# Third mixer of a four-mixer block: weight low parts on GpSimd, key factors in the second memory round, residual rescaling in four parts

## The chip, the cores and the metric

The kernel runs on one core of a Trainium2 chip. The metric is the device time of one execution in microseconds (us). TensorE is PE in the profile, VectorE DVE, ScalarE ACT, GpSimd POOL, SyncE SP.

## The reference

Two blocks of two layers each work on one sequence of 512 tokens with 1024 features, all in float32. The first block has an RG-LRU mixer, a stick-breaking attention, and a SwiGLU feed-forward after each. It ends in an RMS norm with the gain `final_g`. The second block has two gated mixers. The change lies in the first of these, the third mixer of the whole, whose reference is, cut to what matters:

```python
h = rmsnorm(x, norm_gain[l])
mk, mv = jnp.split(memn @ w_mem_kv[l], 2, axis=-1)            # 256 memory rows, 4 heads of 128
qa, ka, va, qb, kb, vb, qm, gate = split_cols(h @ w_in_even[e], SPLIT_EVEN)
qa = rope_2d(rmsnorm(qa, q_norm_a[e]), grid_row, grid_col)    # 8 heads of 64
ka = rope_2d(rmsnorm(ka, k_norm_a[e]), grid_row, grid_col)    # 2 heads of 64
ya = global_gqa(qa, ka, va)                                   # all 512 keys
yb = window_gqa(qb, kb, vb, sink_b[e], rel_bias)              # 128 keys to each side
ym = memory_attn(qm, mk, mv)
y = jnp.concatenate([ya, yb, ym], axis=-1) * jax.nn.silu(gate)
x = x + y @ w_out_even[e]
```

Two things in it matter here. The norm of queries and keys is per head: its sum over 64 features gives one factor for each token and head, by which the keys are scaled before the scores. And the `x` of the residual is the first block's normed output, while the mixer's projections start before that norm's factors are known.

## The kernel before

Activations stand with features on the 128 partitions: a tile is 128 features by 512 tokens, and eight tiles hold one activation. To keep float32 accuracy, each operand of a product is split into a high part (rounded to fp32r) and a low part (the rest), and a product is three matmuls: high by high, high by low, low by high (`mm3`, L169 to L171). One 512-column matmul of each kind follows another.

Weights come in chunks of 128 by 512 (`fetch`): SP issues a load (L149), ACT rounds the high part `wh` (L150), and DVE subtracts to get the low part `wl` (L151). There are six slots of each (`N_W`), and a chunk is fetched five ahead of its use. A projection of 128 output features takes two chunks and 24 matmuls. In the third mixer the weights' key is ("we_m", column): column 0 is the keys `ka`, 1 to 4 the queries `qa`, 5 the window attention's keys `kb`, 6 to 9 its queries `qb`, 10 to 13 the memory queries `qm`, 14 to 17 the memory gates `gm`, 18 to 21 the gates `ga`, 22 to 25 the gates `gb`.

A tile scheduler sets the order in which the instructions stand on each engine; each engine works in that order, and an instruction that waits holds up those behind it.

`even_mixer` runs the third mixer: memory keys and values, the values of both attentions, then `emit("ka", 0)`, `emit("qm", 0)`, and four memory rounds. A round makes scores (`mem_score`: matmuls, maxima L978, exponentials L984, scaling L964), emits the next query's projection, transposes the weights (L1000), emits the gate's projection, and multiplies by the values. Its `between` is what is emitted between transposes and values. Then come four iterations of the global attention ("a"), each with two heads, and four of the window attention ("b"). An iteration makes the scores (L1128, L1129), emits the next query's projection, then transposes of weights (L1151) with evacuations (`evac_split`: ACT L619, DVE L620), the gate's projection, and the products with the values (L1161, L1162), each of which reads an evacuated tile.

A query or key with a norm goes through `rope`: L1065 takes the projection out of PSUM, L1070 to L1072 and POOL's L1073 rotate it, and `factors()` makes the factors: pair sums on PE (L1079), DVE L237, a power on POOL (`rstd`, L239). A query's factors are copied by L1094 and only scale the softmax. The query's low part is a POOL subtract (`split`, L206), and its halves are stacked by SP's DMAs (L550, L551). A key's factors are written out 64 wide by DVE (L1107), transposed by PE (L1111) and multiplied into the keys (L1113), which are then split and stacked by DMAs (L565, L566). `settle` calls this second half: for the keys right before the memory rounds, for each query in the `between` of the iteration before its own.

`rescale_x` brings the residual to the first block's norm: `spread` (PE L252, ACT L257) writes the token factors over all partitions, and eight DVE instructions (L874) scale the eight tiles. It stands right behind the keys' `settle`. The rescaled tiles are read again after both attentions.

Of the kernel before, what the change touches and what calls it, by code (L numbers as in the profile page):

```python
# [9 lines left out]
F32 = mybir.dt.float32  # L10
# [3 lines left out]
ALU = mybir.AluOpType  # L14
# [4 lines left out]
KD = D // 128  # L19
# [46 lines left out]
class Net:  # L66
# [63 lines left out]
    def f(self, n=512):  # L130
        t = self.F.get()
        return t, t[:, 0:n]
# [7 lines left out]
    def fetch(self):  # L140
        nc = self.nc
        key, c0, c1 = self.plan[self.fetched]
        self.fetched += 1
        n = c1 - c0
        src = self.a[key[0]][key[1:]][:, c0:c1]
        w = self.w32.get()
        h = self.wh.get()
        l = self.wl.get()
        nc.sync.dma_start(w[:, :n], src)  # L149
        nc.scalar.copy(h[:, :n], w[:, :n])  # L150
        nc.vector.tensor_tensor(l[:, :n], w[:, :n], h[:, :n].bitcast(F32), op=ALU.subtract)  # L151
        self.w32.put(w)
        self.wh.put(h)
        self.wl.put(l)
        self.ready.append((key, c0, h, l))

    def weights(self, key, c0=0):

        pinned = min(self.pinned, default=len(self.plan))
        while self.fetched < min(len(self.plan), pinned + N_W) and len(self.ready) <= AHEAD:  # L160
            self.fetch()
        self.taken = self.fetched - len(self.ready)
        k, c, h, l = self.ready.popleft()
        assert (k, c) == (key, c0), ((k, c), (key, c0))
        return h, l
# [699 lines left out]
        st["late"] = end  # L865
        return st

    def rescale_x(self, st):
        nc = self.nc
        fg = self.p("final_g", 0, 8)  # L870
        R1 = self.spread(st["r1"], range(4))
        for k in range(KD):
            x = self.X[k][:, 0:512]
            nc.vector.scalar_tensor_tensor(x, x, fg[:, k : k + 1], R1[:, 0:512], op0=ALU.mult, op1=ALU.mult)  # L874
        self.F.put(R1)

    def plan_mem(self, layer):
        for m in range(4):
# [384 lines left out]
    def even_mixer(self, st, gain_next):  # L1263
        nc = self.nc
# [27 lines left out]
        def emit(*want):  # L1292
            kind, i = seq.popleft()
            assert (kind, i) == want
            key = ("we_m", self.even_col(kind, i))
            if kind == "qm":
                got[want] = self.mem_q(key, st)
            elif kind[0] == "g":
                got[want] = self.gate(key, st)
            else:  # L1300
                ps = self.proj(key, st["XH"], st["XL"])
                R = self.row(st)
                if kind == "ka":
                    got[want] = self.gqa_k(ps, R)
                elif kind == "qa":
                    got[want] = self.gqa_q(ps, R)
                else:
                    xt, x = self.f()
                    sc = 0.125 if kind == "qb" else 1.0
                    nc.vector.scalar_tensor_tensor(x, ps, sc, R, op0=ALU.mult, op1=ALU.mult)  # L1310
                    self.P.put(ps)
                    got[want] = self.stack_q(x) if kind == "qb" else self.stack_k(x)
                    self.F.put(xt)
# [3 lines left out]
        def keep(hl):  # L1317
            YH.append(hl[0])
            YL.append(hl[1])

        def gate(key, *more):
            def between():
                emit(*key)
                for f in more:
                    f()
                return got.pop(key)

            return between

        def settle(kind, i):  # L1330
            got[kind, i] = got[kind, i]()

        emit("ka", 0)
        emit("qm", 0)
        settle("ka", 0)
        self.rescale_x(st)
        for i in range(4):
            q = got.pop(("qm", i))
            W = self.mem_score(q, MK[i])
            self.R.put(*q)  # L1340
            emit(*(("qm", i + 1) if i < 3 else ("qa", 0)))
            more = [lambda: settle("qa", 0)] if i == 3 else []
            keep(self.mem_value(W, MV, i, gate(("gm", i), *more)))
        self.R.put(*self.memtiles)
        outs = []

# [4 lines left out]
        for kind, score, value in (("a", self.gqa_score, self.gqa_value), ("b", self.win_score, self.win_value)):  # L1351
            K = got.pop(("k" + kind, 0))
            v = [[t[:, 256 * (kind == "b") + 128 * n :][:, 0:128] for t in V] for n in range(2)]
            for i in range(4):
# [7 lines left out]
                more, after = [], None  # L1362
# [493 lines left out]
```

## Time and profile before

| | |
|---|---|
| time, median of 3 runs | 1895.92 us (1894.84 to 1897.69) |
| profiled execution | 1898.73 us, span 1896.9 us |
| mean granted PE clock | 0.993 of full |
| PE busy | 1857.8 us, 98% of the span |
| DVE busy | 1203.0 us, 63% |
| ACT busy | 888.8 us, 47% |
| POOL busy | 301.5 us, 16% |

The busy time of PE is modelled at the ends of its matmuls and hides short gaps. Where PE waits, the row of the waiting instruction says in brackets how long and for whom. Of the granted clock, 1.00 is 2.4 GHz and 0.50 is 1.2 GHz. In the timeline the third mixer's key factors stand at 1194 us, the memory rounds run from there to about 1262, the global attention to about 1360.

### The profile page before, as it was taken

The page shows a single profiled execution, that of the slowest core. Times are in us where ns is not written, and L with a number is a line of the kernel's source. Part 1 is how long each engine was busy: PE and PEld are TensorE (multiplying, and loading weights), DVE is VectorE, ACT ScalarE, POOL GpSimd, SP SyncE. Part 2 cuts the span into 40 slices and gives each one's busy share as a digit, 9 for nine tenths or more (in the row PEclk, how much of TensorE's full clock was granted, in tenths as well). Part 3 has the DMA queues.
Part 4 walks back from the last instruction along what each step waited for, and adds up shares of the span by engine and source line. Part 5 has one row for each costly group of instructions (what it writes and reads, how often), then busy time and mean ns, then how long its engine had stood idle before and what let it go on. Part 6 is the DMA issues. An engine that isn't in the chain of part 4 may idle for free. (4 is left out here: it accounts for less than half of the span.)

```text
span 1896.9 us, 25808 instructions
## 1 busy us (share of the span) xinstructions
PE 1857.8 (98%) x9003; PEld 1550.5 (82%) x9003; DVE 1203.0 (63%) x2181; ACT 888.8 (47%) x1717; POOL 301.5 (16%) x354
## 2 busy tenths in 40 slices
PE   9989999999999999999999999999999999999998
PEld 6778888888888888788888889888888888888877
DVE  8886555553345998655554345779897655766753
ACT  6774333333335665533333344456665444545542
POOL 2332000000001221200000131222212411322310
PEclk9999999999999999999999999999999999999999
DMA  5333333333335542333333334322443433545522
GB/s 158 109 97 111 95 97 98 96 98 95 97 100 156 141 127 78 101 97 98 96 99 106 108 109 134 92 70 62 114 113 95 127 100 101 145 141 143 140 88 73
DMA packets 124802, 204.04 MB, mean 108 GB/s; under 512 B 21208, under 2 KB 31192, under 8 KB 124672
## 3 DMA queue, kind: packets, MB, share of 16 engines
q1 hardware_dynamic: 124672, 202.39, 37.1%
q8 instruction: 71, 1.16, 0.3%
q14 instruction: 59, 0.48, 0.1%
HBM read 168.76 MB, written 4.40 MB: 91 GB/s over the span
## 5 line engine op out<-in xcount | busy, mean ns | idle before, releaser
L171 PE MATMUL p<-r,wl 128*128 128x512 f32 (+1 forms) x2216 | 854.7, 386 | 9.2 <-DVE wl L151 9.2
L169 PE MATMUL p<-r,wh 128*128 128x512 f32 (+1 forms) x2216 | 857.7, 387 | 2.9 <-ACT wh L150 2.8
L170 PE MATMUL p<-r,wh 128*128 128x512 f32 (+1 forms) x2216 | 852.9, 385 | 0.3 <-POOL r L206 0.3
L150 ACT CAST wh<-w 128x512 fp32r<-128x512 f32 x608 | 371.6, 616 | 642.6 <-PE p L170 481.5
L151 DVE TENSOR_TENSOR wl<-w,wh 128x512 fp32r<-128x512 f32 x608 | 438.4, 725 | 345.8 <-ACT wh L150 345.0
L171 PEld LDWEIGHTS p<-r,wl 128*128 128x128 f32 x2216 | 417.9, 189 | 94.6 <-DVE wl L151 12.0
L169 PEld LDWEIGHTS p<-r,wh 128*128 128x128 f32 x2216 | 418.2, 189 | 86.4 <-ACT wh L150 5.5
L170 PEld LDWEIGHTS p<-r,wh 128*128 128x128 f32 x2216 | 418.1, 189 | 81.4 <-POOL r L206 1.1
L206 POOL TENSOR_TENSOR r<-f,r 128x512 fp32r<-128x512 f32 x102 | 139.8, 1371 | 501.9 <-ACT r L204 501.3
L204 ACT CAST r<-f 128x512 fp32r<-128x512 f32 x146 | 90.6, 621 | 182.5 <-DVE f L531 65.3
L220 POOL TENSOR_TENSOR f<-f,f 128x512 f32<-128x512 f32 x40 | 55.7, 1399 | 477.3 <-ACT f L214 477.2
L505 DVE TENSOR_TENSOR f<-p,f 128x512 f32<-128x512 f32 x68 | 46.9, 690 | 83.3 <-PE p L171 82.4
L620 DVE TENSOR_TENSOR r<-p,r 128x512 fp32r<-128x512 f32 (+2 forms) x152 | 90.4, 638 | 3.8 <-ACT r L619 3.2
L619 ACT CAST r<-p 128x512 fp32r<-128x512 f32 (+2 forms) x152 | 77.2, 557 | 10.7 <-PE p L1151 5.4
L596 PE MATMUL p<-wh,r 128*128 128x512 f32 (+1 forms) x192 | 71.7, 374 | 0.8 <-DVE f L609 0.8
L598 PE MATMUL p<-wh,r 128*128 128x512 f32 (+1 forms) x192 | 71.3, 372 | 0.0
L597 PE MATMUL p<-wl,r 128*128 128x512 f32 (+1 forms) x192 | 71.3, 372 | 0.0
L529 DVE TENSOR_TENSOR f<-p,f 128x512 f32<-128x512 f32 x44 | 30.4, 691 | 63.6 <-PE p L171 63.6
L508 ACT ACTIVATE f<-f 128x512 f32<-128x512 f32 x68 | 43.0, 633 | 38.4 <-DVE f L505 38.4
L964 DVE TENSOR_SCALAR f<-f,s 128x256 f32<-128x256 f32 (+3 forms) x160 | 56.4, 416 | 1.1
L682 DVE TENSOR_TENSOR_SCAN f<-f,f 128x127 f32<-128x127 f32 (+3 forms) x64 | 53.1, 869 | 6.3 <-ACT f L675 6.3
L681 POOL MEMSET f<- 128x1 f32 x64 | 5.2, 100 | 314.1 <-DVE f L509 208.3
(212 smaller groups left out, 1848.3 us busy)
## 6 DMA issues: line engine op xcount, KB each, us to landing
w<-w_gu SPq DMA_DIRECT2D x176, 256.0 KB, 2.9
r<-r SPq DMA_DIRECT2D x240, 128.0 KB, 2.4
w<-w_d SPq DMA_DIRECT2D x80, 256.0 KB, 2.7
w<-wo_m SPq DMA_DIRECT2D x64, 256.0 KB, 2.9
w<-we_m SPq DMA_DIRECT2D x52, 256.0 KB, 2.9
w<-w_rg SPq DMA_DIRECT2D x32, 256.0 KB, 2.9
w<-w_sqk SPq DMA_DIRECT2D x32, 256.0 KB, 2.9
w<-we_o SPq DMA_DIRECT2D x24, 256.0 KB, 2.6
```

The source lines that it names most:

```text
L150: nc.scalar.copy(h[:, :n], w[:, :n])
L151: nc.vector.tensor_tensor(l[:, :n], w[:, :n], h[:, :n].bitcast(F32), op=ALU.subtract)
L169: mm(out, wh, xh, start=start, stop=False)
L170: mm(out, wh, xl, start=False, stop=False)
L171: mm(out, wl, xh, start=False, stop=stop)
L204: nc.scalar.copy(h, src)
L206: e.tensor_tensor(l, src, h.bitcast(F32), op=ALU.subtract)
L596: mm(o, xh, h[:, s], start=st, stop=False)
L597: mm(o, xh, l[:, s], start=False, stop=False)
L598: mm(o, xl, h[:, s], start=False, stop=sp)
L619: nc.scalar.copy(h[:, :n], ps[:, :n])
L620: nc.vector.tensor_tensor(l[:, :n], ps[:, :n], h[:, :n].bitcast(F32), op=ALU.subtract)
```

## The change

Three edits, all in the third mixer.

`fetch` gives the subtract that makes a weight's low part to POOL instead of DVE for the columns 1 to 9 and 18 to 25, that is for `qa`, `kb`, `qb`, `ga` and `gb`: 17 columns of two chunks, 34 instructions. The memory queries and gates and the keys `ka` stay with DVE.

The keys' `settle` moves from ahead of the memory rounds into the `between` of the second round, behind its gate's projection.

`rescale_x` is cut in four: the spread is made at the end of the first round, and each round ends with the rescaling of two tiles.

```diff
--- before.py
+++ after.py
@@ -148,11 +148,17 @@
         l = self.wl.get()
         nc.sync.dma_start(w[:, :n], src)
         nc.scalar.copy(h[:, :n], w[:, :n])
-        nc.vector.tensor_tensor(l[:, :n], w[:, :n], h[:, :n].bitcast(F32), op=ALU.subtract)
+        e = nc.gpsimd if self.low_on_pool(key) else nc.vector
+        e.tensor_tensor(l[:, :n], w[:, :n], h[:, :n].bitcast(F32), op=ALU.subtract)
         self.w32.put(w)
         self.wh.put(h)
         self.wl.put(l)
         self.ready.append((key, c0, h, l))
+
+    @staticmethod
+    def low_on_pool(key):
+
+        return key[0] == "we_m" and (1 <= key[1] <= 9 or key[1] >= 18)
 
     def weights(self, key, c0=0):
 
@@ -865,14 +871,11 @@
         st["late"] = end
         return st
 
-    def rescale_x(self, st):
-        nc = self.nc
+    def rescale_x(self, R1, tiles):
         fg = self.p("final_g", 0, 8)
-        R1 = self.spread(st["r1"], range(4))
-        for k in range(KD):
+        for k in tiles:
             x = self.X[k][:, 0:512]
-            nc.vector.scalar_tensor_tensor(x, x, fg[:, k : k + 1], R1[:, 0:512], op0=ALU.mult, op1=ALU.mult)
-        self.F.put(R1)
+            self.nc.vector.scalar_tensor_tensor(x, x, fg[:, k : k + 1], R1[:, 0:512], op0=ALU.mult, op1=ALU.mult)
 
     def plan_mem(self, layer):
         for m in range(4):
@@ -1332,15 +1335,18 @@
 
         emit("ka", 0)
         emit("qm", 0)
-        settle("ka", 0)
-        self.rescale_x(st)
+        R1 = None
         for i in range(4):
             q = got.pop(("qm", i))
             W = self.mem_score(q, MK[i])
             self.R.put(*q)
             emit(*(("qm", i + 1) if i < 3 else ("qa", 0)))
-            more = [lambda: settle("qa", 0)] if i == 3 else []
+            more = {1: [lambda: settle("ka", 0)], 3: [lambda: settle("qa", 0)]}.get(i, [])
             keep(self.mem_value(W, MV, i, gate(("gm", i), *more)))
+            if i == 0:
+                R1 = self.spread(st["r1"], range(4))
+            self.rescale_x(R1, (2 * i, 2 * i + 1))
+        self.F.put(R1)
         self.R.put(*self.memtiles)
         outs = []
```

The change moves lines: L149 and L150 stay, L151 becomes L152, `mm3` L175 to L177, L206 L212, L237 L243, L239 L245, L505 L511, L509 L515, L620 L626, L874 L878, L964 L967, L978 L981, and from there on each line stands 3 further (L1079 is L1082, L1094 L1097, L1111 L1114).

The scheduler's order at the three places which the prediction speaks of, before and after. The numbers in the names are tiles; the same slot has other numbers from program to program, but not within a piece.

PE before, at the pair sums of the keys (L1079), the spread (L252) and the factors' transposes (L1111). What stands between them is one chunk's first three matmuls and the first scores (128x256):

```order
L170 MATMUL p_119<-r_179,wh_224 128x512
L171 MATMUL p_119<-r_145,wl_230 128x512
L1079 MATMUL p_121<-pair,f_215 128x2 x4
L252 MATMUL p_117<-ident,k_112 128x128 x4
L169 MATMUL p_120<-r_143,wh_225 128x512
L170 MATMUL p_120<-r_162,wh_225 128x512
L171 MATMUL p_120<-r_143,wl_231 128x512
L169 MATMUL p_116<-r_185,r_138 128x256
L170 MATMUL p_116<-r_193,r_138 128x256
L169 MATMUL p_115<-r_185,r_138 128x256
L1111 MATMUL p_122<-ident,f_214 128x128 x4
```

PE now, at the same pair sums (L1082), in the second memory round, behind the last matmul of its gate's projection:

```order
L176 MATMUL p_120<-r_179,wh_226 128x512
L177 MATMUL p_120<-r_145,wl_232 128x512
L1082 MATMUL p_118<-pair,f_215 128x2 x4
L175 MATMUL p_121<-r_161,r_140 128x512
L176 MATMUL p_121<-r_160,r_140 128x512
L177 MATMUL p_121<-r_161,r_141 128x512
L175 MATMUL p_121<-r_148,r_174 128x512
L176 MATMUL p_121<-r_149,r_174 128x512
L177 MATMUL p_121<-r_148,r_168 128x512
L175 MATMUL p_122<-r_155,r_189 128x256
L1114 MATMUL p_119<-ident,f_213 128x128 x4
```

Between the pair sums and the transposes (L1114) there stand now the six products of the memory values and one matmul of the third round's scores.

POOL now, at the power of the keys' factors (L245, s_84) in the same round; before, the power followed POOL's L1073 of the keys without anything between them:

```order
L212 TENSOR_TENSOR r_153<-f_205,r_189 128x512
L152 TENSOR_TENSOR wl_231<-w_2_222,wh_225 128x512
L152 TENSOR_TENSOR wl_232<-w_0_220,wh_226 128x512
L245 TENSOR_TENSOR s_84<-s_83,mhalf 128x8
L212 TENSOR_TENSOR r_166<-f_214,r_181 128x512
```

Two of the weight low parts (L152) stand ahead of the power, and the second, wl_232, has the slot that the last matmul ahead of the pair sums reads.

DVE before, at the key factors and the rescaling (f_206 is the spread):

```order
L151 TENSOR_TENSOR wl_230<-w_1_221,wh_224 128x512
L1107 COPY f_214<-s_78 128x512
L874 SCALAR_TENSOR_TENSOR f_194<-f_194,par,f_206 128x512
L874 SCALAR_TENSOR_TENSOR f_195<-f_195,par,f_206 128x512
L1113 TENSOR_TENSOR f_212<-p_122,f_212 128x512
L874 SCALAR_TENSOR_TENSOR f_196<-f_196,par,f_206 128x512
```

DVE now, from behind the last product of the first memory round to the second round's scaling:

```order
L878 SCALAR_TENSOR_TENSOR f_194<-f_194,par,f_216 128x512
L878 SCALAR_TENSOR_TENSOR f_195<-f_195,par,f_216 128x512
L981 TENSOR_REDUCE s_81<-p_121 128x2
L981 TENSOR_REDUCE s_82<-p_122 128x2
L982 TENSOR_SCALAR s_81<-s_81 128x2
L878 SCALAR_TENSOR_TENSOR f_196<-f_196,par,f_216 128x512
L982 TENSOR_SCALAR s_82<-s_82 128x2
L878 SCALAR_TENSOR_TENSOR f_197<-f_197,par,f_216 128x512
L878 SCALAR_TENSOR_TENSOR f_198<-f_198,par,f_216 128x512
L965 RECIPROCAL s_80<-s_80 128x4
L878 SCALAR_TENSOR_TENSOR f_199<-f_199,par,f_216 128x512
L967 TENSOR_SCALAR f_208<-f_208,s_80 128x256 x2
```

Six of the eight L878 stand now between the first round's product and the L967 that the second round's transposes read; before, all eight stood ahead of the first round's maxima.

POOL before, in the second iteration of the global attention, at the next query's L1073 (f_216) and its power (s_71):

```order
L239 TENSOR_TENSOR s_106<-s_105,mhalf 128x8
L206 TENSOR_TENSOR r_154<-f_203,r_155 128x512
L1073 TENSOR_TENSOR f_216<-f_216,f_204 128x512
L206 TENSOR_TENSOR r_141<-f_216,r_140 128x512
L239 TENSOR_TENSOR s_71<-s_70,mhalf 128x8
```

POOL now, at the same place:

```order
L245 TENSOR_TENSOR s_106<-s_105,mhalf 128x8
L212 TENSOR_TENSOR r_154<-f_213,r_155 128x512
L152 TENSOR_TENSOR wl_233<-w_1_221,wh_227 128x512
L152 TENSOR_TENSOR wl_234<-w_2_222,wh_228 128x512
L152 TENSOR_TENSOR wl_229<-w_0_220,wh_223 128x512
L1076 TENSOR_TENSOR f_212<-f_212,f_202 128x512
L212 TENSOR_TENSOR r_141<-f_212,r_140 128x512
L152 TENSOR_TENSOR wl_230<-w_1_221,wh_224 128x512
L245 TENSOR_TENSOR s_71<-s_70,mhalf 128x8
```

Three low parts stand now ahead of the query's L1076, and one between its low part (L212) and the power (L245).

DVE before, in the same iteration, at the query's factors (L1094) and the evacuations (L620) that the products read:

```order
L620 TENSOR_TENSOR r_182<-p_117,r_165 128x512
L151 TENSOR_TENSOR wl_234<-w_2_222,wh_228 128x512
L151 TENSOR_TENSOR wl_229<-w_0_220,wh_223 128x512
L505 TENSOR_TENSOR f_214<-p_116,f_209 128x512
L237 TENSOR_SCALAR s_70<-p_121 128x8
L620 TENSOR_TENSOR r_183<-p_115,r_190 128x512
L509 SCALAR_TENSOR_TENSOR f_214<-f_202,f_214 128x512
L1094 TENSOR_SCALAR s_69<-s_71 128x8
L620 TENSOR_TENSOR r_142<-p_118,r_156 128x512
L620 TENSOR_TENSOR r_146<-p_119,r_157 128x512
L620 TENSOR_TENSOR r_153<-p_122,r_189 128x512
```

DVE now, at the same place:

```order
L1074 SCALAR_TENSOR_TENSOR f_212<-f_212,par,f_207 128x512
L626 TENSOR_TENSOR r_160<-p_119,r_161 128x512
L626 TENSOR_TENSOR r_153<-p_122,r_189 128x512
L626 TENSOR_TENSOR r_182<-p_117,r_165 128x512
L511 TENSOR_TENSOR f_216<-p_116,f_209 128x512
L243 TENSOR_SCALAR s_70<-p_121 128x8
L1097 TENSOR_SCALAR s_69<-s_71 128x8
L626 TENSOR_TENSOR r_183<-p_115,r_190 128x512
L515 SCALAR_TENSOR_TENSOR f_216<-f_204,f_216 128x512
L626 TENSOR_TENSOR r_142<-p_118,r_156 128x512
L626 TENSOR_TENSOR r_188<-p_119,r_138 128x512
L626 TENSOR_TENSOR r_187<-p_122,r_150 128x512
```

The two weight low parts are gone from DVE, and four evacuations stand behind L1097 where three stood behind L1094.

## Rows read from the trace of the kernel before

**Rows 1.** The page, part 1: busy us (share of the span) and instructions by engine
```profile
PE 1857.8 (98%) x9003; PEld 1550.5 (82%) x9003; DVE 1203.0 (63%) x2181; ACT 888.8 (47%) x1717; POOL 301.5 (16%) x354
```

**Rows 2.** The page, part 5: line engine op, tiles xcount | busy, mean ns | idle before
```profile
L151 DVE TENSOR_TENSOR wl<-w,wh 128x512 fp32r<-128x512 f32 x608 | 438.4, 725 | 345.8 <-ACT wh L150 345.0
...
L206 POOL TENSOR_TENSOR r<-f,r 128x512 fp32r<-128x512 f32 x102 | 139.8, 1371 | 501.9 <-ACT r L204 501.3
```

**Rows 3.** PE's waits, 1140 to 1490 us: who waited for whom: total us, times, longest
```profile
PE p L1128 <- DMA r<-r: 2.7, 2, 1.5
PE p L1111 <- DVE f L1107: 1.8, 1, 1.8
PE p L1162 <- DVE r L620: 1.1, 2, 0.6
PE p L1229 <- DVE f L964: 1.1, 2, 0.8
PE p L1240 <- DVE r L620: 0.9, 3, 0.4
...
PE p L171 <- DVE wl L151: 0.6, 1, 0.6
```

**Rows 4.** Stretches: us, busy PE PEld DVE ACT POOL, PEclk, DMA share, GB/s
```profile
1199.20:1202.60 3.40, 3.40 (x17) 3.40 (x18) 2.67 (x5) 0.62 (x1) 0.12 (x1) 0.50 0.00 0
...
1255.00:1350.00 95.00, 91.20 (x465) 75.17 (x464) 88.94 (x192) 60.60 (x130) 24.80 (x17) 1.00 0.25 72
```

**Rows 5.** Timeline at the key factors: start us, us, engine line op, tiles [idle before]
```profile
1194.23 0.95 PE L1079 MATMUL p<-pair,f 128*128 128x2 f32 x8
...
1194.25 0.62 ACT L150 CAST wh<-w 128x512 fp32r<-128x512 f32 x1 [2.10 <-PE p L170]
...
1195.15 0.62 ACT L204 CAST r<-f 128x512 fp32r<-128x512 f32 x1 [0.29 <-DVE f L954]
...
1197.46 1.26 POOL L206 TENSOR_TENSOR r<-f,r 128x512 fp32r<-128x512 f32 x1
...
1197.53 1.48 DVE L1107 COPY f<-s 128x512 f32<-128x512 f32 x1 [1.54 <-POOL s L239]
...
1199.06 1.97 PE L1111 MATMUL p<-ident,f 128*128 128x128 f32 x8 [1.84 <-DVE f L1107]
...
1201.67 5.09 DVE L874 SCALAR_TENSOR_TENSOR f<-f,par,f 128x512 f32<-128x512 f32 x6
...
1206.69 1.27 DVE L978 TENSOR_REDUCE s<-p 128x2 f32<-128x512 f32 x2
...
1211.63 2.15 DVE L964 TENSOR_SCALAR f<-f,s 128x256 f32<-128x256 f32 x4
...
1213.58 0.44 PE L1000 MATMUL p<-ident,f 128*128 128x128 f32 x2 [0.83 <-DVE f L964]
```

**Rows 6.** Timeline in the first attention, from its first to its third iteration
```profile
1279.57 1.68 DVE L151 TENSOR_TENSOR wl<-w,wh 128x512 fp32r<-128x512 f32 x1
...
1282.00 1.65 POOL L239 TENSOR_TENSOR s<-s,mhalf 128x8 f32<-128x8 f32 x1 [1.30 <-DVE s L237]
...
1304.52 2.00 POOL L206 TENSOR_TENSOR r<-f,r 128x512 fp32r<-128x512 f32 x1 [0.73 <-ACT r L204]
...
1306.48 1.65 POOL L239 TENSOR_TENSOR s<-s,mhalf 128x8 f32<-128x8 f32 x1
...
1308.16 0.17 DVE L1094 TENSOR_SCALAR s<-s 128x8 f32<-128x8 f32 x1 [0.74 <-POOL s L239]
...
1308.24 1.88 DVE L620 TENSOR_TENSOR r<-p,r 128x512 fp32r<-128x512 f32 x3
...
1310.25 0.40 PE L1129 MATMUL p<-r,r 128*128 128x512 f32 x1
...
1310.49 0.39 PE L1162 MATMUL p<-r,r 128*128 128x512 f32 x1
...
1330.65 1.64 POOL L239 TENSOR_TENSOR s<-s,mhalf 128x8 f32<-128x8 f32 x1
```

## The prediction

> **What bounds the kernel now.** I read the page's first part, its costliest groups, the waits of PE around the third mixer, a table of stretches, and last the timeline at the two places that the change touches. The page says that PE is busy for 98% of the span while VectorE (DVE) has 63% and GpSimd (POOL) 16% [rows 1]: only the little time in which PE waits can be won, and any new wait of PE is lost in full. A weight low part costs DVE 0.73 us and frees it of as much; POOL's subtract of the same size and types takes 1.37 on average [rows 2]. Between 1140 and 1490 us PE waits for DVE, or for a DMA behind it, in seven groups that add up to 9.0 us; six are shown, and the seventh, 0.8, is the L1000 of the timeline. The largest are 2.7 for the stacked queries and 1.8 for the key factors [rows 3]. One stretch is slow without being idle: from 1199.2 to 1202.6 the granted clock is 0.50, the lower level, right after the 1.84 us in which PE waited for L1107 [rows 4, 5]. From 1255 to 1350, the first attention, PE is busy for 91.2 of 95 us and DVE for 88.9 [rows 4]. DVE is the near bound there, and POOL, busy for 24.8, has room on average; what decides is where in its queue the new work stands.
>
> **The change part by part.** The times below are set against the profiled execution (1898.73 us, span 1896.9) and then moved to the median, which is 2.8 below it.
>
> *Key factors leave the place ahead of the memory rounds.* PE no longer waits 1.84 for L1107. The slow stretch of 3.40 us at 0.50 would take half as long at 1.00, 1.7; I take 1.5, since its edges are not all work. Gain 3.4.
>
> *What is late next there.* The first scores read the low part of the first memory query. Its cast ends at 1195.15 + 0.62 = 1195.77, but POOL subtracts at 1197.46, because the power of the key factors stands ahead [rows 5]. With that gone the subtract of 1.26 ends at about 1197.1. PE, without the pair sums in its way, is there between 1196.0 and 1196.6: the cast of the weights ends at 1194.25 + 0.62 = 1194.87, and three products at 0.24 (1310.25 to 1310.49 in [rows 6]) and three of half the width follow, with the weight's own low part in between. A wait of 0.5 to 1.1 that the old stall covered: +0.75.
>
> *The same chain in the second round.* The order of PE shows seven matmuls behind the pair sums there, six of 512 and one of 256 columns, before L1114 needs the factors. With the pair sums starting at T, PE is done at T + 0.95 + 6 x 0.24 + 0.12 = T + 2.5. POOL's queue has two low parts ahead of the power, and the second, wl_232, takes the slot which the last product ahead of the pair sums has just read. Its cast can't start sooner: in the trace the cast at the same place began at 1194.25, with the pair sums at 1194.23 [rows 5]. So cast until T + 0.64, low part 1.28 until T + 1.9, power 1.65 [rows 6] until T + 3.6, copy 0.3 (L1107 ended 1199.01, 0.29 after the POOL subtract that it stood beside, [rows 5]) and hand-overs: T + 4.0. PE waits 1.5. Bounds: 0, if the cast and the subtract are early, and 3.0, if the clock falls again for another 1.5. I take 1.5, by the row. The eight DMA issues that stack the keys move with it, past weight loads on SP; the keys are read first in the attention, after 1255, and the weights are loaded five chunks ahead, so the issues cost nothing; without that cover eight of some 0.5 us would hold up a load.
>
> *Rescaling in four parts.* The eight L874 were 1.40 + 5.09 for six [rows 5]; beside the first scores they kept the first maxima (L978) until 1206.69, and the transposes waited 0.83 for L964 at 1213.58 [rows 5]. Now none stands ahead of the first round's maxima, which can take away those 0.8. But by the order of DVE six of them (the first two, late, and the second, third part) stand between the first round's last product and the second round's L967. The row has 3.67 us between the start of L964 and the end of the maxima's first part (1211.63 less 1206.69 + 1.27) in which DVE can do them; six at 0.7 to 0.85 need 4.2 to 5.1, so 0.6 to 1.5 too much. With the spread's copy and one subtract of POOL among them the end is 2.3. Bounds -0.8 and +2.3; I take 1.5, by the row where they last 0.85. The memory rounds together: -3.4 + 0.75 + 1.5 + 1.5 = +0.35 (-3.7 to +3.0).
>
> *Low parts on POOL, first attention.* Each iteration ends in a chain: queries' pair sums, L237, power, L1094, and the evacuations L620 behind it, for which the last products L1162 wait. In the second iteration the power ran from 1306.48, L1094 came at 1308.16, three evacuations took 1.88 (0.63 each), and the last L1162 started at 1310.49 [rows 6]. POOL's order now has a low part (1.28) between the query's subtract and the power, so the power starts at 1307.76 and ends at 1309.41. L1097 holds DVE, which takes its instructions in order, and four evacuations and the second half of the SiLU stand behind it: 0.17 + 4 x 0.63 + 0.68 = 3.4, until 1312.8. PE's order has three score matmuls less ahead of the last L1165, so PE is there at 1310.49 - 3 x 0.24 = 1309.8 and waits 3.0. If the query's subtract falls from 2.00 to 1.28, since DVE's two low parts beside it are gone, 0.7 less: 2.3. The third iteration has the same order, but by the order of before two low parts (0.7 each) stood ahead of its query on DVE, and now none: 1.0 to 3.0 (its power ran from 1330.65 with the same length, [rows 6]). In the first the power found POOL idle for 1.30 [rows 6], which takes the low part in; one more evacuation stands behind L1097, 0.6, or 1.2 if the cast is late: 0 to 1.2. Sum 3.3 to 7.2; I take 5.0, near the middle. What DVE no longer does lies beside work that nobody waits for: it covers nothing here, as the query's power waits for POOL.
>
> *The rest.* In the window attention and its first queries and keys, 18 low parts leave DVE (0.7 each). PE's waits for DVE that they can shorten are 1.1 (L1229), 0.9 (L1240) and 0.6 (L171) [rows 3]. Against it, one POOL low part of 1.28 can hold up a DVE instruction that works from SBUF: a low part on DVE took 1.68 instead of 0.73 beside POOL's L206 (1279.57, [rows 2, 6]). From -2.6 to +3; I take -1.0.
>
> The Trainium skill ("SBUF — State Buffer", Who interferes with whom) says that GpSimd has no port of its own, and that it and a VectorE instruction with two SBUF inputs exclude each other for the whole instruction. The 1.68 agrees with it. If, by this rule, each of the 18 met such an instruction, the rest would stand at its upper end, +3, and the sum at 8.35: 1904.3 instead of the number below.
>
> Sum: 0.35 + 5.0 - 1.0 = +4.35, that is 1903.1 for the profiled execution and **1900.3** at the median.
>
> **The rivals.** *Balance.* DVE is relieved more than I count: L1065 and the evacuations come sooner by one or two low parts of 0.7 in each iteration, which takes back most of the 5.0 when the power's queue is ready early; with the casts early the second round's wait is short too. -1.0 + 5.0 - 3 x 1.4 + 0.35 = about 0: 1896. For it speaks that DVE is busy for 88.9 of 95 us there; against it, that the power depends on POOL, whose queue got longer.
>
> *Faster.* The stall goes for good (-3.4 + 0.75), and L1162's waits of 1.1 go with half of the 2.7 at L1128 [rows 3], since DVE is free when it is asked: -5.1, 1890.8. It decides whether the power starts no later after the pair sums than now; in the second round of the attention the order puts a low part in between, which speaks against it, unless the scheduler's order leaves POOL idle there as in the first.
>
> *The clock falls in the attention.* The gap of 1.84 was followed by the stretch at 0.50, the longest of 1.5 (L1128, [rows 3]) by none: 1255 to 1350 has a clock of 1.00 [rows 4]. Two new waits of 2.3 to 3.0 and the 1.5 of the keys could each bring such a stretch, 1.5 apiece: 4.35 + 3 x 1.5 = +8.9, 1904.8. The Trainium skill ("TensorE: Matmul & The Clock Gate", HAM oscillation) describes waits in a loop that throw the clock back; [rows 4] show it once here.
>
> **How the numbers follow.** Chances: the forecast 0.46 (its own range +0.5 to +10, 1896.4 to 1906), balance 0.24, faster 0.24, the clock 0.06. The 80% range reaches from just below the faster rival, 1890, to the sum of the upper ends, 3.0 + 7.2 + 3 = +13, less its last microsecond: 1908. A measurement of this kernel can tell 0.2% from no change, 3.8 us. Slower by more than that: 0.38 of the forecast's 0.46 and the clock's 0.06, 0.44. Faster: 0.22 of the faster case and 0.03 of the balance, 0.25. The rest, 0.31, lies within.
>
> **What would show it.** In the profile of the changed kernel: no wait of PE at the key factors ahead of the first scores and a clock of 1.00 there; a wait of 1 to 2 us at L1114 in the second round; POOL's rows with L152 between L212 and L245; L1097 some 1.2 us later behind its pair sums in the second and third iteration, and PE waiting for L626 at L1165 for 2 to 3 us. I am wrong if PE waits there no longer than before, if L245 follows the pair sums as soon as now, or if PE's waits between 1190 and 1450 are down by more than 3 us in sum.

## The result, and the profile after

The changed kernel takes 1912.11 us (median of 4 runs, 1911.99 to 1912.82) against 1896.81 for the kernel before in the same comparison: a ratio of 1.0079 (95% interval 1.0067 to 1.0092), 15 us slower. The forecast was 1900.3, with 1890 to 1908 as range: the direction was right, the size was not.

The page's first part hardly shows it. Against [rows 1], PE's share is the same (it is busy 6 us longer), DVE is 9 us lower and POOL 44 higher:

```profile
PE 1863.8 (98%) x9003; PEld 1551.1 (81%) x9003; DVE 1193.9 (63%) x2147; ACT 888.3 (47%) x1717; POOL 345.9 (18%) x388
```

PE's waits, in total us, times and longest, from 1140 to 1500 us of the changed kernel, show where to look; L1165 and L1114 answer to L1162 and L1111 of [rows 3]:

```profile
PE p L1165 <- DVE r L626: 7.9, 7, 2.6
PE p L1243 <- DVE r L626: 2.1, 5, 0.7
PE p L1003 <- DVE f L967: 1.7, 2, 0.8
PE p L1114 <- DVE f L1110: 1.6, 1, 1.6
PE p L1164 <- ACT r L625: 1.2, 1, 1.2
...
PE p L177 <- POOL r L212: 0.6, 1, 0.6
```

The third mixer in three stretches, each cut at the same work in both kernels: from the keys' place to the first attention's first scores, from there to the window attention's first transposes, and from there to the next norm's sums. Columns as in [rows 4]. Before:

```profile
1194.20:1263.00 68.80, 64.63 (x330) 54.49 (x328) 49.99 (x95) 32.02 (x73) 17.56 (x13) 0.98 0.29 83
1263.00:1370.30 107.30, 104.96 (x538) 86.83 (x538) 98.94 (x222) 69.38 (x151) 22.78 (x16) 1.00 0.31 85
1370.30:1505.00 134.70, 132.12 (x671) 111.19 (x672) 108.47 (x226) 77.22 (x181) 37.29 (x52) 1.00 0.37 106
```

And after:

```profile
1194.20:1263.20 69.00, 64.00 (x329) 52.66 (x327) 45.58 (x84) 31.96 (x73) 26.54 (x20) 1.00 0.27 82
1263.20:1382.80 119.60, 110.11 (x536) 89.57 (x536) 94.48 (x206) 69.01 (x151) 46.23 (x35) 0.96 0.27 78
1382.80:1520.30 137.50, 133.97 (x673) 111.49 (x674) 108.24 (x218) 77.40 (x181) 48.90 (x60) 1.00 0.34 101
```

The memory rounds cost 0.2, the first attention 12.3, the rest of the mixer 2.8: 15.3 in all, and the span is 13.3 longer, since the work behind it took 2 us less in this execution. In the first attention the mean clock is 0.96; three stretches of it are at the lower level. One of them:

```profile
1314.70:1318.10 3.40, 3.26 (x8) 2.58 (x9) 1.87 (x4) 0.58 (x1) 0.00 (x0) 0.50 0.00 0
```

The second iteration's timeline shows how a wait comes about; it answers to [rows 6]:

```profile
1304.07 0.65 ACT L150 CAST wh<-w 128x512 fp32r<-128x512 f32 x1
...
1304.79 1.90 POOL L152 TENSOR_TENSOR wl<-w,wh 128x512 fp32r<-128x512 f32 x1 [2.23 <-ACT wh L150]
...
1306.64 1.28 POOL L1076 TENSOR_TENSOR f<-f,f 128x512 f32<-128x512 f32 x1
...
1307.83 0.17 DVE L243 TENSOR_SCALAR s<-p 128x8 f32<-128x8 f32 x1
...
1308.65 1.29 POOL L212 TENSOR_TENSOR r<-f,r 128x512 fp32r<-128x512 f32 x1 [0.73 <-ACT r L210]
...
1309.89 1.29 POOL L152 TENSOR_TENSOR wl<-w,wh 128x512 fp32r<-128x512 f32 x1
...
1311.14 1.65 POOL L245 TENSOR_TENSOR s<-s,mhalf 128x8 f32<-128x8 f32 x1
...
1312.82 0.17 DVE L1097 TENSOR_SCALAR s<-s 128x8 f32<-128x8 f32 x1 [4.82 <-POOL s L245]
...
1313.64 0.50 PE L1165 MATMUL p<-r,r 128*128 128x512 f32 x1 [2.43 <-DVE r L626]
...
1314.10 1.88 DVE L626 TENSOR_TENSOR r<-p,r 128x512 fp32r<-128x512 f32 x3
...
1314.84 0.79 PE L1165 MATMUL p<-r,r 128*128 128x512 f32 x1 [0.47 <-DVE r L626]
```

L243 has the power's input ready at 1308.0, but POOL waits for a cast that its own late rotation (L1076) held up, does a query's low part and then a weight's, and starts the power 3.1 us later. DVE, which the change was to relieve, stands idle for 4.82 us at L1097, an instruction of 0.17, with four evacuations behind it, and PE waits 2.43 and 0.47 for these. From the start of the first attention DVE waited like this for 16.2 us, in four places:

```profile
DVE s L1097 <- POOL s L245: 16.2, 4, 4.8
```

In the kernel before, the same four waits were:

```profile
DVE s L1094 <- POOL s L239: 3.4, 4, 1.2
```

### The profile page after: what moved, and what is told of

Same layout as the page of the kernel before. It is cut to its first block, busy times and chain, and to the rows that moved or that the text cites. A ratio compares the mean times of both kernels' runs of the same rounds, so it can differ in the third digit from the quotient of the medians.

```text
span 1910.2 us, 25806 instructions
## 1 busy us (share of the span) xinstructions
PE 1863.8 (98%) x9003; PEld 1551.1 (81%) x9003; DVE 1193.9 (63%) x2147; ACT 888.3 (47%) x1717; POOL 345.9 (18%) x388
## 5 line engine op out<-in xcount | busy, mean ns | idle before, releaser
L177 PE MATMUL p<-r,wl 128*128 128x512 f32 (+1 forms) x2216 | 854.0, 385 | 9.8 <-DVE wl L152 9.8
L175 PE MATMUL p<-r,wh 128*128 128x512 f32 (+1 forms) x2216 | 857.2, 387 | 0.9 <-ACT wh L150 0.8
L150 ACT CAST wh<-w 128x512 fp32r<-128x512 f32 x608 | 371.4, 615 | 636.7 <-PE p L176 478.4
L152 DVE TENSOR_TENSOR wl<-w,wh 128x512 fp32r<-128x512 f32 x574 | 414.2, 725 | 339.0 <-ACT wh L150 338.0
L177 PEld LDWEIGHTS p<-r,wl 128*128 128x128 f32 x2216 | 417.6, 188 | 95.1 <-DVE wl L152 12.8
L175 PEld LDWEIGHTS p<-r,wh 128*128 128x128 f32 x2216 | 417.9, 189 | 84.4 <-ACT wh L150 3.3
L212 POOL TENSOR_TENSOR r<-f,r 128x512 fp32r<-128x512 f32 x102 | 138.6, 1361 | 461.4 <-ACT r L210 454.7
L511 DVE TENSOR_TENSOR f<-p,f 128x512 f32<-128x512 f32 x68 | 46.9, 690 | 83.8 <-PE p L177 83.1
L626 DVE TENSOR_TENSOR r<-p,r 128x512 fp32r<-128x512 f32 (+2 forms) x152 | 90.4, 639 | 5.7 <-ACT r L625 5.3
L967 DVE TENSOR_SCALAR f<-f,s 128x256 f32<-128x256 f32 (+3 forms) x160 | 64.4, 466 | 1.1
```

Source lines behind the costliest of these rows:

```text
L152: e.tensor_tensor(l[:, :n], w[:, :n], h[:, :n].bitcast(F32), op=ALU.subtract)
L175: mm(out, wh, xh, start=start, stop=False)
L177: mm(out, wl, xh, start=False, stop=stop)
L212: e.tensor_tensor(l, src, h.bitcast(F32), op=ALU.subtract)
L626: nc.vector.tensor_tensor(l[:, :n], ps[:, :n], h[:, :n].bitcast(F32), op=ALU.subtract)
```

## The experiments

Each time is the median of a run's rounds beside runs of the kernel before on the same chip; ratios are to that kernel (1897.42 us for the first eight, 1898.47 for the last two), with 95% intervals.

**The two halves apart.** `low_parts_only` keeps the keys' `settle` and the rescaling where they were; `memory_rounds_only` has in `low_on_pool`:

```diff
-        return key[0] == "we_m" and (1 <= key[1] <= 9 or key[1] >= 18)
+        return False
```

> The 34 low parts on POOL; the keys' factors and the rescaling stay where they were before. Queue theory (POOL's low parts delay the power of the queries' factors, L1097 waits for it at the head of DVE's queue, the evacuations behind it come late, PE waits at L1165 and its clock falls): the cost sits in the first attention, the memory rounds were worth about 0 (first scores at 1263.2 us against 1263.0), so 1910 to 1914 us and three stretches at clock 0.50 in the first attention. Rival, the memory rounds (the moved key factors and rescaling shift everything behind them): 1896 to 1900.

> The keys' factors in the second round and the rescaling in four parts; all low parts stay on DVE. Queue theory: 1895 to 1899 us, no stretch at 0.50 in the first attention; PE still waits 1 to 2 us at the key factors' transposes in the second round. Rival, the memory rounds: 1905 or more.

The low parts alone: 1912.13, ratio 1.0075 (1.0062 to 1.0089). The memory rounds alone: 1896.61, 0.9992 (0.9984 to 1.0001). So the low parts carry all of the loss; whether through POOL's queue or through the ports this pair does not tell. Their first attention (the low parts alone, then the memory rounds alone):

```profile
1261.40:1380.10 118.70, 108.95 (x537) 88.50 (x537) 94.58 (x206) 69.05 (x151) 46.14 (x35) 0.97 0.29 79
```

```profile
1263.20:1370.40 107.20, 104.81 (x538) 86.90 (x538) 98.93 (x222) 69.30 (x151) 22.77 (x16) 1.00 0.31 85
```

One expectation was missed. In `memory_rounds_only` PE does not wait at the key factors' transposes at all: what PE waits for from 1140 to 1263 us is

```profile
PE p L1003 <- DVE f L967: 1.6, 2, 0.8
PE p L177 <- POOL r L212: 0.6, 1, 0.6
```

That does not put the 1.6 at L1114 of the changed kernel down to the low parts: the factors' copy (L1110) starts 3.64 after the pair sums there and 3.30 here, only 0.34 sooner. What covers the wait here is PE's order, in which ten matmuls of the third round's scores stand ahead of L1114, against one in the changed kernel. The low parts alone had only two stretches at 0.50 in the first attention, not three.

**Fewer low parts.** `window_low_parts_only` leaves `kb`, `qb` and `gb` on POOL, `late_window_low_parts` only `qb` 1 to 3 and `gb`:

```diff
-        return key[0] == "we_m" and (1 <= key[1] <= 9 or key[1] >= 18)
+        return key[0] == "we_m" and (5 <= key[1] <= 9 or key[1] >= 22)
```

```diff
+        return key[0] == "we_m" and (7 <= key[1] <= 9 or key[1] >= 22)
```

> The whole change, but of the low parts only the 18 of kb, qb and gb go to POOL. By the order this leaves one low part between a query's subtract and its power, in the second iteration of the first attention, where there were three in the first three. Queue theory: one wait of about 3 us and one stretch at 0.50 there, +3 to +5, and about +2 in the window attention: 1900 to 1904 us. Rival, the ports (every POOL low part holds up DVE, wherever it stands): 18 of 34 times 15.3, +8: 1905 or more, without a single place.

> The whole change, but of the low parts only those of qb 1 to 3 and of gb go to POOL. By the order none then stands in POOL's queue around the powers of the first attention. Queue theory: the first attention takes what it took before (107 us from its first scores to the window attention's first transposes) at a clock of 1.00, and only the window attention's +2.8 stays: 1898.5 to 1900.5 us. Rival, the ports everywhere: 14 of 34 low parts, +6: 1903.

The first took 1907.21, 1.0045 (1.0032 to 1.0058): more than the queue theory said, and in the range of the ports rival. The places speak for the queue all the same: its first attention is 6.0 longer than before, with waits at L1165 of 5.0 in five places, the longest of 2.33 in the second iteration, where the one low part stood behind a query's subtract. A second one of 1.50 in the third iteration I had not counted. Its cause is not shown: POOL stood idle for 3.05 ahead of that iteration's rotation (L1076), and the power's copy came 4.9 after the pair sums, where it was 5.8 before; but four evacuations stood behind it, where three did before. The clock fell once, behind the wait of 1.50. The second kernel took 1901.38, 1.0016 (1.0007 to 1.0025), between the two ranges. Its two stretches:

```profile
1262.70:1371.00 108.30, 105.06 (x537) 86.56 (x537) 97.64 (x216) 69.17 (x151) 30.44 (x22) 1.00 0.30 86
1371.00:1508.40 137.40, 133.93 (x672) 111.43 (x673) 108.89 (x218) 77.16 (x181) 48.45 (x60) 1.00 0.35 102
```

With no low part around a power, the first attention is 1.0 longer than before, all of it in the fourth iteration (38.2 against 37.3); the window's 2.7 stays.

**The wait taken away, the low parts left.** `scale_on_pool` is the changed kernel with

```diff
-            self.nc.vector.tensor_scalar(r8, factors(), 0.125, None, op0=ALU.mult)
+            self.nc.gpsimd.tensor_scalar(r8, factors(), 0.125, None, op0=ALU.mult)
```

> The whole change, and L1097 (128x8, times 0.125) is issued on POOL right behind the power instead of on DVE. PE's and ACT's order stay word for word; DVE loses four tiny instructions. The power itself is as late as after. Queue theory: DVE no longer waits there, PE's waits at L1165 fall from 7.9 us to under 2, and the clock stays at 1.00 in the first attention: 1898 to 1903 us. Rival, the ports: POOL's low parts are all still there, so 1910 to 1914.

1903.57, ratio 1.0026 (1.0017 to 1.0035): 8.5 us of the 15 (10 by the ratios) are gone by moving four instructions of 128x8 from the head of DVE's queue, with all 34 low parts still on POOL and every power as late as after. Time and waits lie just above what was expected (1903 and 2). Its two stretches, and PE's waits in the first of them:

```profile
1265.20:1374.00 108.80, 104.99 (x536) 86.43 (x536) 95.92 (x201) 68.99 (x151) 49.03 (x39) 1.00 0.31 86
1374.00:1511.40 137.40, 133.85 (x672) 111.42 (x673) 108.85 (x218) 77.41 (x181) 48.49 (x60) 1.00 0.36 102
```

```profile
PE p L1165 <- DVE r L626: 2.0, 3, 0.9
PE p L1164 <- ACT r L625: 1.5, 1, 1.5
```

The first attention falls from 119.6 to 108.8, 1.5 above before, and stays at 1.00; the window attention doesn't change. This tells the queue from the ports for the larger part of the first attention's loss. What is left is more than 1.5: with the scaling on POOL but no low parts there (`memory_rounds_scale_on_pool`, below) the first attention took 105.6, so the low parts still cost 3.2 in it.

**The clock.** `pe_filled_in_the_gap` adds, in the second head's first product, before PE's wait (the lines that set `self.filler` by iteration are left out):

```diff
                 O.append(self.P.get())
+                for _ in range(self.filler):
+                    nc.tensor.matmul(O[0][:, 0:256], self.identb, self.sbmask, start=True, stop=True)
```

> The whole change, and PE runs 11, 21 and 21 extra matmuls of 256 columns in bfloat16, whose sums are thrown away, right ahead of the place where it waits in the first three iterations of the first attention (about 1.2, 2.3 and 2.3 us; the waits there were 1.3, 2.4 and 2.6). If the clock falls because PE is idle there, the three stretches at 0.50 go and nothing else changes: 1912.1 less three times 1.5, 1907 to 1909 us. Rival, the clock falls for another reason (DVE's or POOL's load, or the total of waits): the stretches stay and the extra work costs nothing or more: 1911 to 1915.

1914.69, ratio 1.0090 (1.0076 to 1.0105): no gain, and not told apart from the 1.0079 of the change. The timeline shows the filling and, behind it, a wait of 0.24 where 2.43 stood, and the stretch is at 1.00 throughout:

```profile
1311.65 2.47 PE L1164 MATMUL p<-sbmask,identb 128*128 128x256 bf16 x21
...
1314.59 0.50 PE L1167 MATMUL p<-r,r 128*128 128x512 f32 x1 [0.24 <-DVE r L626]
```

```profile
1265.20:1382.80 117.60, 112.51 (x589) 90.94 (x589) 94.45 (x206) 68.96 (x151) 46.23 (x35) 1.00 0.28 80
```

So PE's idling in those places is what the lower clock followed: filled, the three stretches are gone from this execution. The length of a wait does not decide it, though: no such stretch follows the wait of 2.50 in the fourth iteration of this same execution, nor the 2.33 in `window_low_parts_only`, while one follows the 1.30 in the first iteration of the changed kernel. And the clock is worth little. From first scores to first scores (in the last row to the window's first transposes) the iterations took, in us:

| iteration | before | after | after, filled | scale on POOL |
|---|---|---|---|---|
| 1 | 23.6 | 26.2 | 25.6 | 22.7 |
| 2 | 23.0 | 27.7 | 26.5 | 24.1 |
| 3 | 23.4 | 27.8 | 26.5 | 24.1 |
| 4 | 37.3 | 37.9 | 39.0 | 37.9 |

The clock's part is 0.6 + 1.2 + 1.3 = 3.1 of the 12.3, and 1.1 of that was given back in the fourth iteration, where PE waited 2.5 for an ACT cast behind a late weight load. That the last products are paced by DVE's evacuations, so that a faster PE waits more, fits this but was not tested by itself. The expected 1907 to 1909 took 1.5 for each stretch; the first attention gave back 2.0 in all, and this execution was 2.0 longer ahead of the first attention and 2.7 behind the mixer, in work that the filling does not touch. Why the time did not fall at all stays open.

**The window attention.** `idle_subtracts_on_pool` is `memory_rounds_only` with, in `fetch`:

```diff
+        if key[0] == "we_m" and (7 <= key[1] <= 9 or key[1] >= 22):
+            for q in range(2):
+                hf = h[:, 256 * q : 256 * q + 256].bitcast(F32)
+                nc.gpsimd.tensor_tensor(self.sbmask, hf, hf, op=ALU.subtract)
```

> memory_rounds_only (all low parts on DVE), and for the 14 chunks of qb 1 to 3 and gb POOL subtracts the high part from itself into a tile that nobody reads, twice 128x256 for each chunk. POOL works as long as with the low parts, but nobody waits for it. Ports (for the window attention's +2.8): DVE's L967 there gets slower as in the change (0.55 to 0.67 us for 384 columns, 0.42 to 0.56 for 256) and PE waits: 1899 to 1901 us against 1896.6 for memory_rounds_only. Rival, the queue (the low parts come late from POOL, or hold the load's slot): nothing is late here, 1896 to 1897.5.

1903.44, ratio 1.0024 (1.0013 to 1.0035), 3.2 per mille above `memory_rounds_only`. The order of PE, DVE, ACT and SP is the same; only POOL has more work, and the time goes up by some 6 us, beyond the 1899 to 1901 expected for the ports. That nobody waits for this work is not quite so: at 1420.2 ACT waits 1.6 for one of the subtracts, which still reads the slot of the next high part. By then PE was already 2.7 behind `memory_rounds_only`, of the 3.5 that this stretch costs. Its window stretch:

```profile
1371.80:1510.00 138.20, 133.89 (x672) 111.37 (x673) 112.37 (x226) 77.31 (x181) 48.25 (x68) 1.00 0.37 103
```

The scaling of the weights there (busy us, mean ns of one), before, after, and with the idle subtracts:

```profile
L964 DVE TENSOR_SCALAR f<-f,s 128x384 f32<-128x384 f32 x16 | 8.1, 546 | 0.0
L964 DVE TENSOR_SCALAR f<-f,s 128x256 f32<-128x256 f32 x15 | 6.3, 418 | 0.2
```

```profile
L967 DVE TENSOR_SCALAR f<-f,s 128x384 f32<-128x384 f32 x16 | 10.1, 675 | 0.0
L967 DVE TENSOR_SCALAR f<-f,s 128x256 f32<-128x256 f32 x15 | 8.4, 558 | 0.3
```

```profile
L971 DVE TENSOR_SCALAR f<-f,s 128x384 f32<-128x384 f32 x16 | 9.5, 635 | 0.0
L971 DVE TENSOR_SCALAR f<-f,s 128x256 f32<-128x256 f32 x15 | 7.0, 466 | 0.2
```

These means hide two kinds. Of 128x384, most take 0.41 us in all three kernels, and some that run beside a POOL instruction 1.45 to 1.48: two before, four after. Of 128x256 it is 0.35 or 1.38 to 1.39: one before, three after. Four blocked ones more, by about 1.03 each, are the whole rise of 4.1 us. With the idle subtracts it is two and one of these, and six more at 0.70 to 0.77.

POOL's work beside DVE slows DVE's work from SBUF and so costs time by itself, 3.5 in this stretch where the change cost 2.8. For the window attention the ports are thus shown to be enough. That they are the whole of the change's 2.8 is not shown: with the low parts on POOL the order of PE, DVE and ACT in that stretch is another, and DVE has 8 low parts fewer.

**The fourth iteration.** `scale_on_pool_qb2_on_dve` is `scale_on_pool` with:

```diff
+        return key[0] == "we_m" and (1 <= key[1] <= 9 or key[1] >= 18) and key[1] != 8
```

> scale_on_pool, with the two low parts of qb 2 back on DVE. In the fourth iteration of the first attention a weight load was issued 2 us later against the products than before, ACT waited 2.7 for it and PE 1.5 for ACT. Slot theory (POOL's low part of that chunk keeps the load's slot): the load is earlier and most of the 1.5 goes, 1901.5 to 1902.5 us. Rival, the order of SP (the load stands behind the bias rows and the stacked queries in any case): 1903 to 1904.

1902.18, ratio 1.0023 (1.0014 to 1.0031) against 1.0026 for `scale_on_pool`: not told apart, and PE's wait for ACT there went from 1.5 to 1.1 only. The time lies in the slot theory's range, but by the waits that theory falls for the larger part; what makes that load late, the order on SP or another thing, stays open. It is 0.6 us of the 12.3.

**Is there something to win?** The same move of the scaling in the kernel before, and with the memory rounds of the change:

> The kernel before, with the query factors' scaling (128x8) on POOL behind the power instead of on DVE. Queue theory: DVE stood idle 1.2, 0.7 and 0.6 us for the power in before as well, and PE waited 1.1 for L1162: -0.5 to -2, 1895 to 1897 us. Rival (that wait of DVE was covered): 1897 to 1898, no difference.

> The memory rounds of the change without its low parts on POOL, and the query factors' scaling on POOL. Queue theory: the sum of memory_rounds_only (-0.8) and before_scale_on_pool (-0.5 to -2): 1894.5 to 1896.5 us. Rival (the waits in the memory rounds and in the attention take each other's place): 1896 to 1898.

1896.53, 0.9989 (0.9980 to 0.9998), and 1896.20, 0.9991 (0.9982 to 0.9999). PE's waits at the evacuations (1.1 in [rows 3]) are gone in both, and the first attention takes 105.6 in both, against 107.3. By the ratios both are some 2 us faster than the kernel before, at the edge of what can be told, and the two gains don't visibly add.

## Why the prediction was right in kind and wrong in size

*The memory rounds: right.* Forecast +0.35, measured +0.2 in the profile and 0.9992 alone. The old stall and its slow stretch are gone (0.98 to 1.00 in the first stretch). Each term came near its place: L177 waits 0.6 for the query's low part (taken: 0.75), L1114 1.6 (taken: 1.5), the rounds' L1003 1.7 instead of 0.8 (taken: +1.5, so high by about 0.6). With the gain of 3.4 as taken, these measured terms add up to -0.3, so that the sum came within 0.2 is partly luck.

*The place and chain of the loss: right.* POOL's queue delays the power, L1097 holds DVE, four evacuations and the SiLU stand behind it, PE waits at L1165. The steps have their sizes: the power's copy came 1312.82 - 1306.36 = 6.46 after the pair sums

```profile
1306.36 0.95 PE L1082 MATMUL p<-pair,f 128*128 128x2 f32 x8
```

where 1308.16 in [rows 6] was 5.11 after its own pair sums:

```profile
1303.05 0.95 PE L1079 MATMUL p<-pair,f 128*128 128x2 f32 x8
```

The forecast had 1309.41 and so 6.36.

*The step that failed is the sum for the first attention.* It took 5.0 out of 3.3 to 7.2, and the stretch measured 12.3: 8.6 for the first three iterations without the clock, 3.1 for the clock, 0.6 for the fourth iteration. Three things were missing. First, I let the lower end count for half: the query's subtract did fall from 2.00 to 1.29, as that end assumed, but the rotation ahead of it had to wait for another low part, whose cast came late and which lasted 1.90, until 1306.64. What one low part gave back another took: the copy came 6.46 after the pair sums, at the upper end's 6.36. So the iterations lost 2.0, 3.5 and 3.1 without the clock, where 0 to 1.2, 2.3 to 3.0 and 1.0 to 3.0 stood. Second, the fourth iteration was priced at nothing; it lost 0.6 to 1.7. Third, the clock was a rival with a chance of 0.06, as if it excluded the waits. It comes on top of them: in the changed kernel each of the three new waits of 1.3 to 2.6 was followed by a stretch at 0.50 (in `low_parts_only` two of three, in `window_low_parts_only` one of two). Its price, though, was 1.0 each, not the 1.5 that I took from a stretch in which PE had no other limit. The Trainium skill ("TensorE: Matmul & The Clock Gate", HAM oscillation) has waits in a loop throw the clock back; the three stretches agree, and they are gone where the gaps were filled; the waits of 2.33 and 2.50 without a stretch show that not every wait does it.

*The window attention: wrong in sign.* I took -1.0, for low parts that leave DVE; it was +2.8. By the windows DVE has 8 instructions fewer there (218 against 226), not 18, as the weights are fetched five chunks ahead, and its busy time is the same (108.2 and 108.5): the scaling (L967) takes 4.1 of the 6.2 us that the low parts gave. I had the upper end of +3 in hand and took the relief instead. The Trainium skill ("SBUF — State Buffer", Who interferes with whom) has the rule that GpSimd shares its port pair with VectorE, and it lists tensor_scalar among the instructions that can take that pair. L967, which goes from 546 to 675 ns, and the idle subtracts agree. Weighing the upper end above my hope for relief would have been right here. In the first attention `scale_on_pool` leaves 3.2 of the low parts' cost (how much of it is the ports' is not told), against 10.8 that went with the wait at L1097.

*The rivals.* Balance and faster both rested on DVE's relief. DVE was indeed relieved, by 4.5 us busy in the first attention, and it spent the time waiting for POOL.

## What to carry to other kernels

Moving work off a busy engine onto an idle one is priced by the queue that it joins: ask what short, urgent instruction stands behind it there, and which in-order engine waits for that one with its own work queued behind. A tiny dependent instruction at the head of a busy engine's queue can cost more than the work that was moved; put it on the engine that makes its input. Add up the consequences of one wait (later evacuations, a lower clock) instead of giving them chances as rivals.

## What was not expected of the hardware

28 extra POOL subtracts of 128x256 whose results nobody reads cost 5 us in the profile against the kernel before (span 1901.9 against 1896.9) and 6 by the ratios against `memory_rounds_only`, for the larger part through a slower DVE. And in the filled kernel the weight load of the fourth iteration began to be issued 1.3 us sooner than in the changed one (1366.38 against 1367.68), but the issue lasted 2.1 us instead of 0.4, and ACT's cast came at 1371.63 in both; why the issue took so long is open.
